# Two weight groups by turns: the first two column groups of the input projection advance together, a quarter of x at a time

## The chip, the core and the metric

One core of a Trainium2 chip runs the program. The metric is device microseconds of one execution, as the median of three runs, and less is better. TensorE (PE in the rows, PEld for its weight loads) does the matrix products, VectorE (DVE), ScalarE (ACT) and GpSimd (POOL) the elementwise work, and SyncE (SP) issues every load from memory.

## The reference, cut to what matters

The reference runs 256 tokens of 2048 features through two blocks of two layers each. Only the start of the first layer (`even_layer`) is touched here:

```
def even_layer(x, norm_g, w_in, ...):
    hn = rmsnorm(x, norm_g)               # x: 256 tokens x 2048 features
    proj = hn @ w_in                      # 2048 x 6144
    q, k, v, u, z_a, z_b = split(proj)    # 1024 columns each
    o_a = chunked_relpos_attention(q, k, v, rel_bias) * silu(z_a)
    y = gelu(s5_ssm(u, ...))              # state space model over u
    o_b = y * sigmoid(y @ w_glu + b_glu) * silu(z_b)
    return x + concat([o_a, o_b]) @ w_out
```

`rmsnorm` multiplies by the gain and divides by the root of the mean square over all 2048 features. The division is one factor for each token, so the kernel applies it to the finished product, not to x.

## The kernel before

**Jobs.** Every matrix product is cut into column groups of 512, and a group into jobs. A job holds two blocks of 128 rows of the weight for 512 columns: 0.5 MB, a tile `raw` of 128x1024 floats. `run` (line 267) goes through the list of jobs in order. A job's weight is loaded by SP, split by ACT into a high part (`hi`, line 214) and by DVE into the rest (`lo`, line 165), and multiplied by PE at line 420. PE does three products for each 128x128 block: x high times weight high, x low times weight high, x high times weight low, so 24 matmuls a job. Job i uses the tiles hi*i* and lo*i*. There are five `raw` buffers and four of `hi` and `lo`. The splits of a job stand up to two jobs ahead of its matmuls in the program (`ahead`, line 313).

**x.** x comes in four quarters of 512 features, and a group of the first layer goes through them in order, two jobs for each. When a job that needs a new quarter is prepared, ACT and DVE split that quarter too (`Act.split`, line 36: four pieces each, ACT `s<-s,e1g` at line 214 and DVE `s<-s,e1g,s` at line 176). Its hook `Norm.add` (line 444) then has ACT square the quarter and POOL add the square to the sum of squares (POOL `s<-s,s` 128x1024 at line 165).

**The norm.** After the fourth quarter the generator `norm_gen` takes over: two additions on DVE fold the sum, PE multiplies it by a matrix of ones (`b<-s,ones`, line 219), DVE forms the mean (`rsv`, line 172), ACT takes the logarithm and the exponential (`rst`, `rsy`, with a table load before each), and three more DVE instructions give the factor of each token, `rsy`.

**Accumulators.** A group's result gathers in one of two PSUM buffers (`ps_main`, bufs=2, names `mm...`). When the last job of a group is done, its `post` function is put on a list and called in `bg_step`; it empties the accumulator on DVE (`s<-mm,rsy`, line 165) and gives `'wait'` back as long as `norm_ok` isn't set. `run` forces background steps before a job while more than one `post` is outstanding. A third group reuses the first one's accumulator.

**Order.** All engines execute their instructions in the order in which the program lists them. Into the stream of jobs `bg_step` mixes background generators: the norm, the preparation of the S5 model (`s5pre`: small instructions of 128x32 on DVE, then additions and products of 128x512), the S5 blocks and the attention. Which instruction they add where follows from estimated costs, not from the chip. The first groups are u0, u1 (the S5 input), q0, k0, v0 and so on; u0 and u1 are also spread over partitions by eight small DMAs each (`stack`, line 726). The first loads are issued by the list `K.first`, where `None` stands for one `raw` and `load(i)` for quarter i of x.

Of the kernel before, what the change touches and what calls it, by code (L numbers as in the profile page):

```python
# [26 lines left out]
class Act:  # L27
    """256 columns of tokens for `n` blocks of 128 features, as two float32r parts."""
# [42 lines left out]
class Kern:  # L71
# [124 lines left out]
    def smax(self, out, a, b, acc):  # L196
        """out = -(a + b); acc = its least, the negative of the greatest of a + b"""
        self._ew('D', self._n(out))
        self.nc.vector.tensor_tensor_reduce(out=out, in0=a, in1=b, op0=OP.add, op1=OP.min,  # L199
                                            scale=-1.0, scalar=3.0e38, accum_out=acc)  # L200
# [26 lines left out]
    def lane(self, gens, width=1, prio=0, name=""):  # L227
        """a queue of (condition, generator maker), `width` of them at a time"""
        L = dict(q=list(gens), live=[], width=width, prio=prio, name=name)
        self.lanes.append(L)  # L230
        self.lanes.sort(key=lambda l: l['prio'])
        return L

    def bg_step(self, force=False):
# [9 lines left out]
        for L in list(self.lanes):  # L244
            while len(L['live']) < L['width'] and L['q'] and L['q'][0][0]():
                L['live'].append(L['q'].pop(0)[1]())
            for g in list(L['live']):
                if not force and max(self.busy.values()) > self.clock + self.SLACK and L['prio'] > 0:
                    return moved
                # not before what it waits for on another engine is done  # L250
# [16 lines left out]
    def run(self):  # L267
# [45 lines left out]
        def ahead(i):  # L313
            """the splits of the jobs after job i, as far as LOOK goes"""
# [12 lines left out]
        for i, j in enumerate(jobs):  # L327
            ahead(i)
            # a raw tile is free again once all of it is read
# [23 lines left out]
        n = 0  # L353
# [5 lines left out]
    def group(self, name, src, acts, orient, post, units, ready=None, bg=False):  # L359
        """one group of 512 columns: `units` is the list of (DRAM AP, kt count)"""  # L360
# [66 lines left out]
def kmap(acts):  # L427
    """k-tile index -> (Act, block in it)"""
    out = []
    for a in acts:  # L430
        out += [(a, i) for i in range(a.n)]
    return out


class Norm:
    """1 / sqrt(mean of squares + eps) for each token, the same on all partitions"""
# [7 lines left out]
    def add(self, src, cols=None):  # L444
        """src: a slot with four blocks of features"""
# [15 lines left out]
    def mean(self, out, extra=None):  # L461
        """generator: out = mean of squares (+ eps), then 1/sqrt"""
# [25 lines left out]
def rsqrt(K, y, v, t):  # L488
    """y = 1 / sqrt(v): a first value by exp(-ln(v) / 2), then a step of Newton"""
# [11 lines left out]
def together(*gens):  # L501
    """the operations of several chains by turns"""
# [9 lines left out]
def steps(n, gen):  # L512
    """n operations at a time"""
# [34 lines left out]
def sincos_ops(K, s, c, x, a, b, d):  # L548
    """sin and cos of x; a, b, d: scratch"""
# [31 lines left out]
    # n mod 4 in -2..2, then a turn by n quarters  # L581
# [10 lines left out]
    K.tt('D', z, z, n, OP.mult)                      # sine of the turn  # L592
    yield
    K.ts('D', r, r, -1.0, 1.0, OP.mult, OP.add)      # cosine of the turn
# [15 lines left out]
def evac_scaled(K, ps, rs, out=None):  # L610
    """a feature-major group times a row of tokens' factors"""
# [13 lines left out]
def evac_silu(K, ps, rs_half, done):  # L625
    """x times sigmoid(x): with h = x / 2 it is (tanh(h) + 1) h"""
# [12 lines left out]
def token_scales(K, rs, out):  # L639
    """generator: factors by token on partitions"""  # L640
# [8 lines left out]
def soft_rows(K, p, nm, sm, cols):  # L649
    """p holds -(s); exp(s - max) with its sums. cols: [(first, end)]"""  # L650
# [4 lines left out]
class E1:  # L655
    """relative-position attention in chunks beside an S5 state space model"""

    def __init__(self, K, D, x_src, out_norm):
# [12 lines left out]
        K.first += [None, lambda: load(0), None, lambda: load(1), None, None, lambda: load(2), lambda: load(3)]  # L671
# [26 lines left out]
    def build(self):  # L698
# [8 lines left out]
        def post_u(i):  # L707
            def f(ps):
                if not self.norm_ok or K.slots.free < 3:
                    return 'wait'  # L710
                # even tokens before odd ones
# [5 lines left out]
                def stack():  # L717
                    """both tokens of a pair on the partitions, for two tiles of states at a time"""
# [66 lines left out]
        def load_bias(hg):  # L785
            def gen():
                [s] = yield from K.gslots(1)
                K.nc.sync.dma_start(s, D['e1_bias'][hg])
                # keys of the chunk after the query's own are out of reach
# [138 lines left out]
        # the first half of y before the second  # L928
# [6 lines left out]
    def s5(self):  # L935
# [30 lines left out]
        def powers():  # L966
            """cosine and sine of 2, 4, .. 128 angles"""
# [9 lines left out]
        def coefs():  # L977
            """A, and the factor of B: (A - 1) / lambda"""
# [20 lines left out]
        def pre():  # L999
# [9 lines left out]
            def times(out, v, re, im, tm):  # L1009
                """a complex number for each state times its coefficients"""  # L1010
# [16 lines left out]
            # cosines and sines of 0, 2, .. 30 times each state's angle  # L1027
# [20 lines left out]
            # y takes the real part: the imaginary parts of C with their sign turned  # L1048
# [7 lines left out]
        def fill(e, pad, src, b):  # L1056
            """block b's coefficients, zero outside of each state's own channels"""
# [11 lines left out]
        def block(b):  # L1069
            def gen():  # L1070
# [7 lines left out]
                # the projections in, the channels of each tile's pairs of tokens on their own rows  # L1078
# [4 lines left out]
                # cosines and sines of 0, 2, .. 254 times each state's angle  # L1083
# [21 lines left out]
                # two tokens a step  # L1105
# [42 lines left out]
                # the even tokens' own inputs: C B  # L1148
# [28 lines left out]
                # gelu by tanh, twice its value  # L1177
# [22 lines left out]
        def yz(i):  # L1200
            def gen():
                # y times silu(z), a quarter of (2 y) (2 silu): y_t is 2 y; sigmoid's half is still to come
# [13 lines left out]
class Layer:  # L1216
    """what the layers share: the norm at their start and the sum with the residual at their end"""
# [15 lines left out]
    def begin(self):  # L1233
        """called when the projection out of the layer before starts"""
# [24 lines left out]
    def take(self, g, ps, xr):  # L1259
        """four blocks of the sum: the residual, and this layer's input"""  # L1260
# [13 lines left out]
def out_proj(K, D, wname, n, acts, xr, nxt, tag):  # L1274
    """xr: list of the residual's slots (filled by the time of use)"""
# [12 lines left out]
def attend(K, S_mm, bias, pv, out, left, done, heads=2):  # L1288
    """generator: two heads at a time, queries on partitions. S_mm(bank, e) emits the scores of head e
    (queries 0..127 with keys 0..127 in columns 0..127, queries 128..255 in columns 128..383)"""  # L1290
# [39 lines left out]
def log1p_ops(K, out, z, s, w, d):  # L1330
    """log(1 + z) for z in 0..1, by the series of atanh(z / (2 + z))"""
# [19 lines left out]
class O1(Layer):  # L1351
# [3 lines left out]
    def build(self):  # L1355
# [11 lines left out]
        # forget gates: 16 columns  # L1367
# [4 lines left out]
        def f_mm(raw, _):  # L1372
# [3 lines left out]
            # four blocks of rows at a time, on a quarter of the columns each  # L1376
# [4 lines left out]
        def f_post():  # L1381
# [6 lines left out]
            def gen():  # L1388
# [8 lines left out]
                K.stt(m, x, -1.0, x, OP.mult, OP.min)            # -|x|  # L1397
# [40 lines left out]
        # the first group before the gates, that the norm has its time  # L1438
# [69 lines left out]
class E2(Layer):  # L1508
    """HGRN2 beside sparse attention (whose blocks and window hold all of the tokens at this length)"""
# [20 lines left out]
    def norm_gen(self):  # L1530
        """the first block's last norm and this layer's, in one factor for each token"""
# [13 lines left out]
    def build(self):  # L1545
# [45 lines left out]
        def hgrn(i):  # L1591
            def gen():
# [6 lines left out]
                # pairs of tokens: (2i, 2i), (2i+1, 2i) and (2i+1, 2i+1) in one product  # L1599
# [112 lines left out]
    def nsa(self, g):  # L1712
# [54 lines left out]
        # the gates: 48 columns  # L1767
# [8 lines left out]
        def g_mm(raw, k0):  # L1776
# [4 lines left out]
            # two blocks of rows at a time, on half of the columns each  # L1781
# [8 lines left out]
        def g_post():  # L1790
# [6 lines left out]
            def gen():  # L1797
# [3 lines left out]
                # both halves' sum, tokens on the partitions  # L1801
# [9 lines left out]
                # no block is complete before token 31  # L1811
# [12 lines left out]
        # compressed keys and values: an MLP over blocks of 32 tokens  # L1824
        def c_mm(n, j, x):
            def f(raw, _):
# [6 lines left out]
                # even steps on the first half of the columns, odd ones on the second  # L1833
# [50 lines left out]
        # two steps after each group from the third on  # L1884
# [29 lines left out]
        def first_rows():  # L1914
            # the first 128 tokens' values, and the compressed ones, as two float32r parts
# [15 lines left out]
        def head(i, e):  # L1931
# [3 lines left out]
            def gen():  # L1935
# [19 lines left out]
                # the columns that no key has  # L1955
# [74 lines left out]
class O2(Layer):  # L2030
    """a short convolution and a gated linear recurrence"""
# [4 lines left out]
    def build(self):  # L2036
# [6 lines left out]
        # columns: four taps, their sum's bias, the gates' biases, lambda  # L2043
# [5 lines left out]
        def pre():  # L2049
# [3 lines left out]
            K.stt(v[0], lam, -1.0, lam, OP.mult, OP.min)                      # -|lambda|  # L2053
# [352 lines left out]
```

## Time and profile before

| what | value |
|---|---|
| median of 3 runs | 2395.09 us (2394.77 to 2395.71) |
| span of the profiled execution | 2394.8 us |
| PE busy | 2336.9 us, 98% of the span |
| DVE busy | 1585.9 us, 66% |
| ACT busy | 1152.5 us, 48% |
| POOL busy | 386.8 us, 16% |
| chain that ended last | PE 84%, DVE 8%, POOL 2%, issue 2%, ACT 2%, DMA 1% |

PE is busy nearly all of the time, and 84% of the chain that ended last is PE's. A shorter run can come only from the idle time of PE (58 us in all, span less busy time) or from its clock. The profiled execution's span is 0.3 us under the median; no other time is given for that execution. Matmuls overlap, so PE's pace is read from the distance between starts, not from the duration of one matmul.

### The profile page before, as it was taken

How to read it: one execution, taken by the hardware profiler on the slowest of the kernel's cores; microseconds unless marked ns; L12 is line 12 of the kernel's file. 1: busy time of each engine (PE TensorE's matmuls, PEld its weight loads, DVE VectorE, ACT ScalarE, POOL GpSimd, SP SyncE). 2: the span in 40 equal slices, each digit the busy share in tenths (PEclk: the TensorE clock that was granted, in tenths of full speed). 3: DMA queues.
4: the chain of work that ended last, by engine and by line, in shares of the span. 5: the costliest groups of instructions: out<-in, count | busy, mean ns of one | idle time of the engine just before them, and what ended most of it. 6: DMA issues, size and time to landing. Idle time of an engine off the chain costs nothing.

```text
span 2394.8 us, 47663 instructions
## 1 busy us (share of the span) xinstructions
PE 2336.9 (98%) x19906; PEld 2253.3 (94%) x19906; DVE 1585.9 (66%) x2409; ACT 1152.5 (48%) x1662; POOL 386.8 (16%) x320
## 2 busy tenths in 40 slices
PE   7999999999999999999999999999999999999997
PEld 7989998999999999989999999899999999999997
DVE  7978878675554545676758574566667446777764
ACT  5354454444444344543445443455555434666643
POOL 1111211010000000123324253101110000111210
PEclk9999999999999999999999999999999999999999
DMA  6544454555545555554544454554444555555453
GB/s 225 191 152 149 142 177 153 175 186 164 193 160 175 174 170 185 169 177 156 170 160 159 162 165 159 192 178 142 142 142 143 195 183 180 165 175 168 161 196 111
DMA packets 116167, 402.23 MB, mean 168 GB/s; under 512 B 14832, under 2 KB 17776, under 8 KB 115952
## 3 DMA queue, kind: packets, MB, share of 16 engines
q1 hardware_dynamic: 115952, 399.19, 50.7%
q8 instruction: 156, 2.56, 0.4%
q14 instruction: 59, 0.48, 0.1%
HBM read 396.00 MB, written 2.10 MB: 166 GB/s over the span
## 4 chain that ended last, share of the span: by engine, by line
PE 84%; DVE 8%; POOL 2%; issue 2%; ACT 2%; DMA 1%; DVEq 0%; SPq 0%; ACTq 0%; POOLq 0%
PE mm L420 75%; PE b L219 6%; DVE lo L165 3%; DVE s L165 2%; POOL s L165 2%; DVE s L194 1%; DVE s L176 1%; PE b L224 1%; PE b L420 1%; ACT s L214 1%; ACT hi L214 1%; DMA raw<-in_e_in 1%; PE b L1836 0%; DVE s L170 0%; DMA s<-in_e_bias 0%
## 5 line engine op out<-in xcount | busy, mean ns | idle before, releaser
L420 PE MATMUL mm<-s,hi 128*128 128x256 f32 x9984 | 1830.5, 285 | 10.4 <-ACT s L214 7.6
L420 PEld LDWEIGHTS mm<-s,hi 128*128 128x128 f32 x9984 | 1563.9, 193 | 18.3 <-ACT s L214 8.0
L420 PE MATMUL mm<-s,lo 128*128 128x256 f32 x4992 | 1418.6, 284 | 24.5 <-DVE lo L165 24.4
L165 DVE TENSOR_TENSOR lo<-raw,hi 128x1024 fp32r<-128x1024 f32 x730 | 934.0, 1294 | 622.2 <-ACT hi L214 620.4
L214 ACT ACTIVATE hi<-raw 128x1024 fp32r<-128x1024 f32 x730 | 756.9, 1054 | 646.1 <-PE mm L420 557.5
L420 PEld LDWEIGHTS mm<-s,lo 128*128 128x128 f32 x4992 | 960.8, 192 | 28.9 <-DVE lo L165 28.8
L165 POOL TENSOR_TENSOR s<-s,s 128x512 f32<-128x512 f32 (+1 forms) x128 | 273.9, 2154 | 1411.4 <-ACT s L214 586.9
L214 ACT ACTIVATE s<-s 128x1024 f32<-128x1024 f32 (+6 forms) x188 | 132.9, 713 | 263.3 <-DVE s L165 137.2
L420 PE MATMUL mm<-hi,s 128*128 128x512 f32 x768 | 244.6, 394 | 0.0
L219 PE MATMUL b<-s,s 128*32 128x32 f32 (+8 forms) x3008 | 175.0, 244 | 4.8 <-POOL s L186 2.1
L420 PEld LDWEIGHTS mm<-hi,s 128*128 128x128 f32 x768 | 145.0, 189 | 30.8 <-ACT s L214 0.3
L219 PEld LDWEIGHTS b<-s,s 128*32 128x32 f32 (+2 forms) x2976 | 148.3, 135 | 23.4 <-POOL s L186 2.5
L420 PE MATMUL mm<-lo,s 128*128 128x512 f32 x384 | 150.5, 392 | 1.6 <-DVE lo L165 1.6
L214 ACT ACTIVATE s<-b 128x384 f32<-128x384 f32 (+6 forms) x135 | 57.2, 462 | 134.9 <-PE b L219 92.7
L165 DVE TENSOR_TENSOR s<-s,s 128x512 f32<-128x512 f32 (+8 forms) x134 | 85.8, 666 | 45.7 <-ACT s L214 44.5
L420 PEld LDWEIGHTS mm<-lo,s 128*128 128x128 f32 x384 | 72.6, 189 | 16.7 <-DVE lo L165 2.4
L176 DVE SCALAR_TENSOR_TENSOR s<-s,s 128x1024 f32<-128x1024 f32 (+3 forms) x76 | 82.6, 1089 | 3.1 <-ACT s L214 2.2
L214 ACT ACT_TABLE_LOAD x44 | 56.5, 1283 | 16.1 <-DVE s L176 14.7
L204 DVE COPY_PREDICATED s<-hmask,b 32x64 f32<-32x64 int32 (+1 forms) x144 | 36.0, 250 | 30.4 <-PE b L219 26.6
L214 ACT ACTIVATE s<-s,nsam 128x15 f32<-128x15 f32 (+2 forms) x96 | 37.6, 394 | 36.0 <-DVE nsam L199 36.0
L170 POOL TENSOR_SCALAR s<-alibi 128x256 f32<-128x256 f32 x16 | 17.8, 1111 | 212.3 <-PE b L219 174.1
L186 POOL MEMSET s<- 128x512 f32 (+7 forms) x65 | 25.8, 410 | 123.3 <-DMA s<-in_e_bias 59.1
(148 smaller groups left out, 966.6 us busy)
## 6 DMA issues: line engine op xcount, KB each, us to landing
raw<-in_e_in SPq DMA_DIRECT2D x336, 512.0 KB, 4.1
raw<-in_o_in SPq DMA_DIRECT2D x208, 512.0 KB, 4.0
raw<-in_e_out SPq DMA_DIRECT2D x80, 512.0 KB, 4.2
raw<-in_o_out SPq DMA_DIRECT2D x72, 512.0 KB, 4.4
raw<-in_e_outa SPq DMA_DIRECT2D x16, 512.0 KB, 3.6
raw<-in_o_rg SPq DMA_DIRECT2D x10, 512.0 KB, 3.7
raw<-in_e_glu SPq DMA_DIRECT2D x8, 512.0 KB, 3.8
raw<-in_e_cmp SPq DMA_DIRECT2D x8, 512.0 KB, 5.1
```

The lines of the kernel that those rows point to most:

```text
L165: self._eng(e).tensor_tensor(out, a, b, op=op)
L170: self._eng(e).tensor_scalar(out, a, s1, None, op0=op0)
L176: self.nc.vector.scalar_tensor_tensor(out, a, s, b, op0=op0, op1=op1)
L186: self._eng(e).memset(out, v)
L194: self.nc.vector.tensor_tensor_scan(out, d0, d1, init, op0=OP.mult, op1=OP.add)
L204: self.nc.vector.copy_predicated(out, mask, a)
L214: self.nc.scalar.activation(out, a, func, scale=scale, **kw)
L219: self.nc.tensor.matmul(out, l, r, start=start, stop=stop, skip_group_check=True, **kw)
L224: self.nc.tensor.transpose(out, a, self.ident[:p, :p])
L420: self.nc.tensor.matmul(out, l, r, start=start, stop=stop, skip_group_check=True)
```

## The change

The list of jobs of the first two groups is rearranged, and the list of first loads with it. Comments and docstrings that went away are left out of this diff.

```
-        K.first += [None, lambda: load(0), None, lambda: load(1), None, None, lambda: load(2), lambda: load(3)]
+        K.first += [None, lambda: load(0), None, None, None, lambda: load(1), None, lambda: load(2), lambda: load(3)]
...
         for g, (n, i, o) in enumerate(order):
             K.group(f"e1.{n}{i}", None, acts, o, posts[n](i), units('e1_in', g))
 
+        n = 4 // K.JK
+        j = K.jobs[:8 * n]
+        K.jobs[:8 * n] = [j[g * 4 * n + u * n + i] for u in range(4) for g in range(2) for i in range(n)]
```

JK is 2, so n is 2. Before, jobs 0 to 7 are u0 on the four quarters of x and jobs 8 to 15 are u1. Now jobs 0 and 1 are u0 on the first quarter, 2 and 3 u1 on the first quarter, 4 and 5 u0 on the second, and so on to jobs 14 and 15, u1 on the fourth. Both accumulators are open from job 2 on. The second, third and fourth quarter of x are needed at jobs 4, 8 and 12 instead of 2, 4 and 6. u0 is complete after job 13 instead of job 7; u1 after job 15 in both. Job 16, the first of q0, takes over u0's accumulator in both.

On PE, around the matrix of ones (`b`) and the first matmul of job 16 (`mm53`, in u0's accumulator). Before, where `mm45` is u1:

```order
L420 MATMUL mm45_508<-s32_148,lo8_425 128x256
L219 MATMUL b46_533<-s34_158,ones_79 128x256
L420 MATMUL mm45_508<-s32_148,hi9_464 128x256
...
L420 MATMUL mm45_508<-s42_347,lo15_720 128x256
L420 MATMUL mm53_833<-s32_148,hi16_761 128x256
```

Now, where `mm39` is u1:

```order
L420 MATMUL mm39_262<-s43_586,lo14_675 128x256
L219 MATMUL b49_769<-s34_158,ones_79 128x256
L420 MATMUL mm39_262<-s43_586,hi15_709 128x256
...
L420 MATMUL mm39_262<-s43_586,lo15_710 128x256
L420 MATMUL mm53_852<-s32_148,hi16_739 128x256
```

The ones stood seven jobs ahead of job 16 and now stand one job ahead of it.

On DVE, from the mean to the emptying of u0's accumulator. Before (`mm38` is u0):

```order
L165 TENSOR_TENSOR lo11_544<-raw11_360,hi11_543 128x1024
L172 TENSOR_SCALAR rsv5_86<-b46_533 128x256
L165 TENSOR_TENSOR rst6_87<-rsv5_86,rsy7_88 128x256
L176 SCALAR_TENSOR_TENSOR rst6_87<-rst6_87,rsy7_88 128x256
L176 SCALAR_TENSOR_TENSOR rsy7_88<-rst6_87,rsy7_88 128x256
...
L165 TENSOR_TENSOR lo13_630<-raw13_428,hi13_629 128x1024
L165 TENSOR_TENSOR s47_659<-mm38_187,rsy7_88 128x4x128x2
```

Now (`mm35` is u0, `mm39` u1; `s46` to `s50` belong to S5):

```order
L165 TENSOR_TENSOR lo17_775<-raw17_599,hi17_774 128x1024
L172 TENSOR_SCALAR rsv5_86<-b49_769 128x256
...
L176 SCALAR_TENSOR_TENSOR rsy7_88<-rst6_87,rsy7_88 128x256
L165 TENSOR_TENSOR s47_669<-s46_668,s11_98 128x512
L165 TENSOR_TENSOR s48_670<-s46_668,s11_98 128x512
L165 TENSOR_TENSOR s47_669<-s47_669,s48_670 128x512
L165 TENSOR_TENSOR lo18_814<-raw18_637,hi18_813 128x1024
...
L165 TENSOR_TENSOR s48_670<-s50_821,s5pw13_100 128x32 x2
...
L165 TENSOR_TENSOR s50_821<-s50_821,s48_670 128x32x4 x2
L165 TENSOR_TENSOR s51_842<-mm35_174,rsy7_88 128x4x128x2
L165 TENSOR_TENSOR s52_844<-mm39_262,rsy7_88 128x4x128x2
```

The mean now stands behind lo17 instead of lo11, and the forced background steps put 18 S5 products and additions of 128x32 to 128x128 between the token factors and the emptying of u0, where before there were two scalings by a half, one `lo` and some small S5 instructions. From the 2939th PE instruction on (job 108) the order of the two kernels is the same.

## Rows read from the trace of the kernel before

**Rows 1.** Waits of PE, 0 to 60 us: total, times, longest.

```profile
PE mm L420 <- DVE lo L165: 4.1, 2, 2.6
```

**Rows 2.** PE's timeline: start and duration in us, in brackets idle time before.

```profile
19.39 0.40 PE L420 MATMUL mm<-s,hi 128*128 128x256 f32 x2
21.25 0.39 PE L420 MATMUL mm<-s,lo 128*128 128x256 f32 x1 [1.46 <-DVE lo L165]
...
24.93 0.39 PE L420 MATMUL mm<-s,hi 128*128 128x256 f32 x1 [0.66 <-DVE s L176]
...
30.82 0.58 PE L420 MATMUL mm<-s,lo 128*128 128x256 f32 x1 [2.64 <-DVE lo L165]
...
43.69 0.60 PE L219 MATMUL b<-s,ones 128*128 128x256 f32 x2
...
64.49 0.40 PE L420 MATMUL mm<-s,hi 128*128 128x256 f32 x2
...
75.41 0.39 PE L420 MATMUL mm<-s,lo 128*128 128x256 f32 x1 [1.83 <-DVE lo L165]
```

**Rows 3.** Two stretches; the figure behind POOL's count (0.52) is the granted clock.

```profile
31.20:34.40 3.20, 3.20 (x17) 3.20 (x17) 3.20 (x11) 0.00 (x0) 0.00 (x0) 0.52 0.77 192
137.00:140.20 3.20, 3.20 (x9) 2.50 (x8) 3.20 (x4) 2.01 (x5) 0.00 (x0) 0.52 0.29 60
```

**Rows 4.** DVE's timeline, 14 to 35 us.

```profile
14.97 1.67 DVE L176 SCALAR_TENSOR_TENSOR s<-s,e1g,s 128x256 fp32r<-128x256 f32 x4
16.55 2.63 DVE L172 TENSOR_SCALAR s<-s 128x32 f32<-128x32 f32 x2
...
22.25 3.82 DVE L176 SCALAR_TENSOR_TENSOR s<-s,e1g,s 128x256 fp32r<-128x256 f32 x4
25.98 3.41 DVE L176 SCALAR_TENSOR_TENSOR s<-s 128x32 f32<-128x32 f32 x6
...
31.78 1.22 DVE L165 TENSOR_TENSOR lo<-raw,hi 128x1024 fp32r<-128x1024 f32 x1
32.92 1.67 DVE L176 SCALAR_TENSOR_TENSOR s<-s,e1g,s 128x256 fp32r<-128x256 f32 x4
34.50 0.28 DVE L176 SCALAR_TENSOR_TENSOR s<-s 128x32 f32<-128x32 f32 x2
```

**Rows 5.** POOL's timeline: the first two of three additions of squares.

```profile
16.42 2.50 POOL L165 TENSOR_TENSOR s<-s,s 128x1024 f32<-128x1024 f32 x1 [13.79 <-ACT s L214]
22.07 2.52 POOL L165 TENSOR_TENSOR s<-s,s 128x1024 f32<-128x1024 f32 x1 [3.15 <-ACT s L214]
```

**Rows 6.** Timeline of DVE and ACT: the norm and the emptying of u0.

```profile
45.52 0.42 DVE L172 TENSOR_SCALAR rsv<-b 128x256 f32<-128x256 f32 x1
47.70 0.42 ACT L214 ACTIVATE rsy<-rst 128x256 f32<-128x256 f32 x1
49.41 0.41 DVE L165 TENSOR_TENSOR s5pw<-s5pw,s 128x32 f32<-128x32 f32 x2
54.24 2.03 DVE L165 TENSOR_TENSOR s<-mm,rsy 128x1024 f32<-128x1024 f32 x1
```

**Rows 7.** DVE's timeline: three S5 instructions; 18 small ones' start; what follows them.

```profile
61.10 2.01 DVE L165 TENSOR_TENSOR s<-s,s 128x512 f32<-128x512 f32 x3
...
76.50 0.71 DVE L165 TENSOR_TENSOR s<-s,s5pw 128x32 f32<-128x32 f32 x4
...
80.15 2.35 DVE L165 TENSOR_TENSOR lo<-raw,hi 128x1024 fp32r<-128x1024 f32 x2
```

**Rows 8.** SP's timeline: the eight DMAs that spread u0.

```profile
58.68 6.64 SPq L726 DMA_DIRECT2D s<-s  x8
```

**Rows 9.** Waits of PE, 136 to 400 us.

```profile
PE mm L420 <- DVE lo L165: 3.2, 3, 1.4
PE b L224 <- POOL s L182: 2.2, 1, 2.2
PE b L219 <- POOL s L186: 2.1, 1, 2.1
```

## Prediction

> **What bounds the kernel now.** I read the page first: PE is busy for 98% of the span, so only its idle time and its clock can give or cost something. Then I read PE's waits in the first 60 us [rows 1], and PE's timeline to see where they lie [rows 2]. After the first load PE stops three times in the first group, u0: 1.46, 0.66 and 2.64 us, 4.76 together. Each ends when DVE delivers a `lo` or a piece of x. After the longest of them PE's clock is granted at 0.52 in the mean of a stretch of 3.2 us, the level of 1.2 GHz, and PE gets 17 matmuls through it [rows 3]. At its usual pace it would be 26: from the ones at 43.69 to job 16 at 64.49 lie 171 PE instructions, 0.122 us each [rows 2], which makes 2.9 us a job. The stretch lasts 3.4 us by the distance of the starts, so it costs about 1.5 us.
>
> Next I read DVE around these waits [rows 4] with POOL beside it [rows 5]. Two instructions of 128x32 take 2.63 us, where a stretch without POOL gives 0.13 each: 11.0 us from 34.50 [rows 4] to 45.52 [rows 6] hold five `lo` of 1.14 (31.78 to 32.92), two foldings of the sum of about 1.1 together (an estimate, from a third of the triple of [rows 7] and half of that) and 32 small ones. Four pieces of x take 3.82 instead of 1.67, six small ones 3.41 instead of 0.8. Each of the three begins just after POOL began to add squares, 2.50 us [rows 5]; the third addition is of the same kind. So each addition cost DVE 2.2 to 2.6 us, 7.1 us together, and this is a good part of why `lo` came late.
>
> **The change, part by part.** No instruction's work goes or comes: 16 jobs, 16 loads, three additions, one norm remain. Three things move.
>
> (a) The quarters of x are needed at jobs 4, 8 and 12 instead of 2, 4 and 6. DVE then has four jobs (11.6 us of PE) for one quarter: four `lo` at 1.14 (4.6), four pieces 1.6 (32.92 to 34.50), some 30 small ones (4) and one blocked addition of at most 2.5 make 12.7 at the worst against 11.6, which the splits that stand two jobs ahead cover for three quarters; before it was the same less two `lo` and half of the small ones, 8.4 against 5.8. The three waits in u0 go, and the half-clock stretch with them. Job 3 starts at 19.39 [rows 2] as before, jobs 3 to 15 and the ones take 13 x 2.9 + 0.25 = 37.9, and PE would reach job 16 at 57.3, 7.2 earlier than its 64.49. The first loads only follow the new need: raw 2 and 3 ahead of the second quarter. Bounds: nothing to 7.2 us; but it is a gain only if job 16 can start then.
>
> (b) Job 16 can't. It writes into u0's accumulator, which DVE must empty first, with factors that come out of the norm, and the norm needs the last quarter of x. Before, u0 was emptied from 54.24 to 56.27 [rows 6], 8.2 us ahead of job 16. Now the chain is this. The ones stand behind job 14 on PE, at 57.3 - 2.9 - 0.25 = 54.1, with 0.6 of duration 54.7. DVE, in order, reaches the mean after 14 `lo` (lo4 to lo17, 16.0), three quarters of x (4.7), 81 small ones (10.5), three triples of 128x512 (5.8, [rows 7] less the overlap) and the two foldings (1.1): 38.1 us. lo4 can start at 16.5 to 17.9: lo2 is done at 14.97 [rows 4], then 14 small ones and lo3 take 2.9, less up to 1.4 because 0.5 MB of x no longer lie ahead of the weight (an estimate from the stretch's load rate; I take 16.5). That gives 54.6 for the mean without any blocking. With it, 0 to 7.1 more; the additions again meet pieces of x and small ones on DVE, but not at the same points, so I take two thirds, 4.9. The mean starts at 59.5, and what PE does before it, waits included, sets nothing any more.
>
> From the mean to the next free slot of DVE it was 3.9 us (45.52 to 49.41, with ACT's logarithm, table load and exponential in it [rows 6]): 63.4. Then, as the program lists them, one triple 1.95, lo18 1.14, two scalings of 128x256 (0.42 at most each, I take 0.6 together), the 18 S5 instructions 3.65 (76.50 to 80.15, [rows 7]) and the emptying itself 2.03 [rows 6]: 72.8. PE stands still from about 57.3 to 72.8, and job 16 starts 8.3 later than before. Queued behind job 16's first matmul are only PE's own jobs 16 and on; ACT's hi20 and on wait for PE in turn, so nothing else gets ahead.
>
> After this stop PE restarts at the lower clock. Before, 2.64 us of idle brought one half-clock stretch, 1.5 us. Nothing before, away from the start, shows a stop of 15 us. Bounds 0 and 3 (two such stretches); I take 1.5, by the nearest row.
>
> The Trainium skill, "SBUF — State Buffer", section "Who interferes with whom", says that a DVE instruction with two SBUF inputs contends with a GpSimd instruction that reads SBUF, and the one that issues second waits it out in full. The rows above agree, with 2.2 to 2.6 us for an addition of 2.5. By that rule all three additions of the new order block in full, 7.4 us in place of my 4.9, and the sum would be 2.5 us larger.
>
> (c) The 16 small DMAs for u0 and u1 are issued together now. Before, SP was tied up for 6.64 us by the first eight [rows 8], the next weight came late, and PE waited 1.83 us at 75.41 [rows 2]. Now eight jobs' weights are issued ahead of them in SP's order, through job 23; both sets end 13.3 us after u0's emptying, at about 86, and job 24 starts not before 72.8 + 8 x 2.9 = 96. This wait goes with its restart: -1.9. If a load then takes over 10 us, it stays.
>
> Sum: +8.3 + 1.5 - 1.9 = +7.9 us on the span of 2394.8: 2402.7, and with the 0.3 by which the median is above the span, 2403.0. The part after 96 us I leave as it is: the S5 blocks move by some jobs against the weights up to job 108, but the waits there hang on the same chains of DVE and POOL.
>
> **Rivals.** A, DVE isn't blocked: the additions fall beside instructions that don't mind. The mean is then at the ones, 54.7, all else 4.8 earlier: +3.1, 2398.2. For it: the new order spaces the additions 11.6 us apart. Against it: in [rows 4] three of three blocked.
>
> B, the other side: S5's new place clears the later waits. From 136 to 400 us PE waits 7.5 us for S5's operands and late `lo` [rows 9], and one such stop is followed by 0.52 of the clock [rows 3]; three groups of them would make 4.5. S5's blocks stand earlier against the weights now, by up to some 140 matmuls in the PE order. Were all of these waits to go, 7.9 - 12.0 = -4.1: 2391.0, not slower. It decides from about 8 us on. Against it: between the first S5 transposes and the first S5 output lie twelve jobs and ten `lo` in both orders, so I see no more room there than before.
>
> C, job 16 doesn't wait, since a free accumulator is found. Then -7.2 - 1.9 = -9.1: 2386.0. Against it: two buffers, both open from job 2 on.
>
> D, S5's new place makes a further group of waits like that at 136 us, 2.1 and 1.5: +11.5, 2406.6. Nothing speaks for or against it.
>
> **How the numbers follow.** This kernel's measurement can tell 0.2%, 4.8 us, from no change. The forecast with its own range (blocking 3 to 7.1, clock 0 to 3: 2399.6 to 2406.7) has 0.52, D 0.08, A 0.17, B 0.19 and C 0.04. Slower by over 0.2% are most of the forecast and D: 0.58. Within are A, two thirds of B and the low end of the forecast: 0.32. Faster are C and the part of B that comes with A: 0.10. The range runs from 2393.5, which takes in A and half of B, to 2408.0, which takes in D with some blocking more.
>
> **What would show it.** Right: no PE wait over 0.7 us between 19 and 54 us and no half-clock stretch there; then one wait of 12 to 17 us on DVE's emptying (`s<-mm,rsy`) right behind the second group, half clock after it, no wait of 1.8 us for job 19, and `rsv` on DVE starting 4 to 6 us after the ones. Wrong: `rsv` within 1 us of the ones (A), PE without a long wait before q0 (C), or the waits of 136 to 400 us gone (B). The forecast as a whole is wrong if job 16 starts before 66 us.

## The result, and the profile after

| | kernel before | changed kernel |
|---|---|---|
| median | 2394.93 us (2390.95 to 2395.71, 4 runs) | 2419.21 us (2418.12 to 2420.26, 4 runs) |
| span of the profiled execution | 2394.8 us | 2417.0 us |
| PE busy | 2336.9 us | 2339.1 us |
| idle time of PE (span less busy) | 57.9 us | 77.9 us |

The changed kernel is slower: ratio 1.0101, 95% interval 1.0087 to 1.0116, or 24.3 us. The forecast of slower was right. 2403.0 was not, and the range, up to 2408, does not hold the time. Of the 22.2 us between the two spans 20.0 are idle time of PE, and 2.2 are more busy time for the same 19906 matmuls.

**The start.** PE's waits in the changed kernel, 0 to 60 us: total, times, longest.

```profile
PE mm L420 <- DVE lo L165: 2.3, 4, 0.7
PE mm L420 <- DVE s L176: 0.6, 2, 0.4
```

The three waits of [rows 1, 2] are gone; what is left are six short ones. Now the timeline of the changed kernel from the ones to job 16, PE first, then DVE (start and duration in us, in brackets idle time before).

```profile
55.99 0.60 PE L219 MATMUL b<-s,ones 128*128 128x256 f32 x2
60.01 0.28 PE L420 MATMUL mm<-s,lo 128*128 128x256 f32 x1
74.62 0.77 PE L420 MATMUL mm<-s,hi 128*128 128x256 f32 x2 [14.33 <-DVE s L165]
...
61.46 0.42 DVE L172 TENSOR_SCALAR rsv<-b 128x256 f32<-128x256 f32 x1
68.91 0.71 DVE L165 TENSOR_TENSOR s<-s,s5pw 128x32 f32<-128x32 f32 x4
72.55 3.76 DVE L165 TENSOR_TENSOR s<-mm,rsy 128x1024 f32<-128x1024 f32 x2
```

The mean (`rsv`) starts 5.5 us after the ones, the 18 small S5 instructions stand ahead of the emptying, and job 16 starts at 74.62 instead of 64.49 [rows 2], 10.1 us later. The clock in four stretches of the changed kernel (busy time and count of PE, PEld, DVE, ACT and POOL, then the granted clock, DMA share and GB/s):

```profile
31.20:34.40 3.20, 3.03 (x25) 2.83 (x25) 3.13 (x9) 1.06 (x1) 0.00 (x0) 1.00 0.30 87
74.60:79.60 5.00, 4.98 (x24) 5.00 (x25) 4.76 (x8) 0.00 (x0) 0.00 (x0) 0.51 0.32 79
206.60:212.30 5.70, 5.01 (x21) 4.72 (x22) 5.49 (x7) 3.02 (x4) 2.65 (x2) 0.50 0.41 132
316.70:321.80 5.10, 5.10 (x22) 4.92 (x23) 3.57 (x10) 3.42 (x10) 0.00 (x0) 0.50 0.31 106
```

The half-clock stretch at 31 us [rows 3] is gone. In its place PE is granted 0.51, the 1.2 GHz level, after the long wait, and two more such stretches lie at 207 and 317 us.

**After 96 us.** In the two traces the last of PE's matmuls that differs is the 3396th, in job 108, at 406 us of the kernel before. PE's waits in the changed kernel, 136 to 400 us, the window of [rows 9].

```profile
PE b L219 <- DVE e1m L199: 6.6, 2, 5.4
PE b L219 <- issue: 5.2, 2, 3.9
PE mm L420 <- DVE lo L165: 2.4, 3, 1.2
PE mm L420 <- ACT hi L214: 1.2, 2, 0.6
PE b L219 <- POOL s L165: 0.9, 1, 0.9
```

They add up to 16.3 us. In the kernel before all waits of this window are 8.4 us, of which [rows 9] shows the three largest, 7.5. And they are other waits: the two rows for POOL there are gone, and the two at the top here are new. "issue" means that the profile gives no releaser for PE. The timeline of the engines around the first of them, 206 us, shows one:

```profile
197.89 0.42 SPq L792 DMA_DIRECT2D s<-in_e_bias  x1
203.00 1.02 POOL L186 MEMSET s<- 64x256 f32 x3 [4.36 <-DMA s<-in_e_bias]
203.79 1.90 ACT L214 ACTIVATE s<-s 64x128 f32<-64x128 f32 x6 [10.28 <-POOL s L186]
205.72 3.90 ACT L214 ACTIVATE hi<-raw 128x1024 fp32r<-128x1024 f32 x4
205.79 0.44 PE L219 MATMUL b<-s,s 128*32 128x32 f32 x16 [3.90 <-issue]
206.83 0.80 PE L420 MATMUL mm<-s,hi 128*128 128x256 f32 x2 [0.59 <-ACT hi L214]
208.09 0.58 PE L420 MATMUL mm<-s,lo 128*128 128x256 f32 x1 [0.46 <-DVE lo L165]
```

POOL's row holds three memsets. The first masks the attention bias and must wait until that bias has come by DMA, at 203 us. The other two clear the tiles of an S5 block and do not need the bias; they only stand behind it on POOL. ACT's six copies fill these tiles, ACT's `hi` stands behind the copies, and PE's 16 matmuls of 128x32 read them: 3.9, 0.6 and 0.5 us of waiting, and half clock after it. Around 317 us:

```profile
310.69 2.34 POOL L165 TENSOR_TENSOR s<-s,s 128x1024 f32<-128x1024 f32 x1 [5.24 <-DVE s L176]
310.84 2.47 DVE L165 TENSOR_TENSOR s<-s 128x256 f32<-128x256 f32 x1
313.34 0.42 ACT L214 ACTIVATE s<-s 128x256 f32<-128x256 f32 x1 [5.13 <-DVE s L165]
314.74 1.32 DVE L165 TENSOR_TENSOR lo<-raw,hi 128x1024 fp32r<-128x1024 f32 x1 [1.43 <-ACT hi L214]
316.67 1.65 PE L219 MATMUL b<-s,s 128*128 128x128 f32 x4 [5.39 <-DVE e1m L199]
```

POOL multiplies the attention output by its gate. The DVE instruction that began 0.15 us later, a step of an S5 block's gelu, takes 2.47 us; ACT's tanh, ACT's `hi`, DVE's `lo`, the row maxima of the attention and PE follow in a chain.

### The profile page after: what moved, and what is told of

It reads as the page before. It is cut to its first block, busy times and chain, and to the rows that moved or that the text cites. A ratio compares the mean times of both kernels' runs of the same rounds, so it can differ in the third digit from the quotient of the medians.

```text
span 2417.0 us, 47650 instructions
## 1 busy us (share of the span) xinstructions
PE 2339.1 (97%) x19906; PEld 2253.2 (93%) x19906; DVE 1586.4 (66%) x2409; ACT 1152.7 (48%) x1662; POOL 384.1 (16%) x320
## 4 chain that ended last, share of the span: by engine, by line
PE 81%; DVE 4%; POOL 2%; issue 1%; ACT 1%; DMA 0%; DVEq 0%; ACTq 0%; SPq 0%; POOLq 0%
PE mm L420 73%; PE b L219 6%; POOL s L165 2%; DVE lo L165 2%; PE b L420 1%; DVE s L165 1%; PE b L224 1%; ACT s L214 1%; DVE s L194 1%; ACT hi L214 1%; DVE s L176 1%; PE b L1840 0%; PE mm L219 0%; DMA s<-in_e_bias 0%; DVE s L199 0%
## 5 line engine op out<-in xcount | busy, mean ns | idle before, releaser
L219 PE MATMUL b<-s,s 128*32 128x32 f32 (+9 forms) x3008 | 177.3, 245 | 16.2 <-issue 6.7
L186 POOL MEMSET s<- 128x512 f32 (+8 forms) x65 | 25.5, 406 | 146.2 <-DMA s<-in_e_bias 74.9
```

What stands on the lines that cost most here:

```text
L186: self._eng(e).memset(out, v)
L219: self.nc.tensor.matmul(out, l, r, start=start, stop=stop, skip_group_check=True, **kw)
```

## The experiments

The ratios are to the kernel before, run on the same chip beside each kernel (its medians there: 2394.6 to 2396.2 us). Experiments 1 to 4 share a chip, 5 to 8 a second and 9 to 11 a third; 12 has a fourth, and the changed kernel of the result was timed apart from them. A difference of two experiments of different sets is therefore given against the kernel before as well, and 2 to 3 us can lie within the intervals. All experiments but the fourth need the S5 and attention steps at chosen jobs. For that the class `Kern` is replaced by one that takes these steps from a list. Filled with a kernel's own places it gives that kernel's own order on every engine.

```
-    K = Kern(tc, ctx, slots=SLOTS)
+    K = Pinned(tc, ctx, slots=SLOTS)
...
+PINNED = [
+    (45,0,0), (45,0,1), (51,0,0), (51,0,1), (53,0,0), (53,0,1), (55,0,0), (57,0,0), (57,0,1), (59,0,0), (59,0,1),
...
+        while self.pin and abs(self.pin[0][0]) <= self.pos:
+            p, name, k = self.pin[0]
```

An entry is twice the job's number plus one, the lane (0 is S5, 1 attention) and which of its blocks. By the traces, experiments 5, 6 and 12 then differ from the changed kernel only in the instructions that were moved, and 9 and 10 likewise from the kernel before.

| kernel | median us | ratio, 95% interval |
|---|---|---|
| 1 changed, S5 steps of before | 2405.97 | 1.0040 (1.0027 to 1.0053) |
| 2 before, S5 steps of changed | 2416.85 | 1.0087 (1.0074 to 1.0101) |
| 3 as 1, prompt emptying | 2399.38 | 1.0014 (1.0005 to 1.0023) |
| 4 changed, old order of loads | 2420.98 | 1.0104 (1.0088 to 1.0119) |
| 5 changed, bias mask later | 2409.01 | 1.0052 (1.0039 to 1.0064) |
| 6 changed, gate on DVE | 2417.31 (1 run) | |
| 7 as 3, two quarters by turns | 2396.00 | 0.9999 (0.9990 to 1.0008) |
| 8 as 1, squares on DVE | 2401.93 | 1.0021 (1.0013 to 1.0030) |
| 9 before, squares on DVE | 2391.44 | 0.9985 (0.9977 to 0.9994) |
| 10 as 9, bias mask later | 2389.77 | 0.9976 (0.9967 to 0.9985) |
| 11 as 7, both edits of 10 | 2390.86 | 0.9978 (0.9969 to 0.9987) |
| 12 changed, 5 and 6 together | 2406.05 | 1.0044 (1.0031 to 1.0058) |

**1. The changed start with the S5 steps where they were.** Expected:

> The changed kernel, with every step of the S5 and attention generators put at the job and in the order that it has in the kernel before (from job 22 on the engines then run the same order of instructions as before). Theory T (the loss has two parts: about 11 us at the start, from the wait for u0's accumulator, and about 12 us after 96 us, from the new place of the S5 steps): the start is as in the changed kernel, with one wait of about 14 us near 60 us, the waits of 3.9 us at 206 and 5.4 us at 317 are gone, and the time is 2406 (2403 to 2409). Rival R (the later loss comes from the late start itself, whatever the order of the steps): the time stays at 2417 to 2420.

Measured 2405.97, as theory T has it. The long wait is there (14.34 us, job 16 at 74.02), and from 136 to 400 us this kernel's PE waits are those of [rows 9] again, 8.3 us in all:

```profile
PE mm L420 <- DVE lo L165: 2.1, 3, 1.0
PE b L219 <- POOL s L186: 2.1, 1, 2.1
PE b L224 <- POOL s L182: 1.8, 1, 1.8
PE b L219 <- ACT s L214: 1.4, 1, 1.4
```

So the start costs 10.7 us (2405.97 less 2395.31), and the other 13 to 14 us (24.3 less 10.7; 13.2 by 2419.21 less 2405.97) come from where the S5 and attention steps stand, not from being late.

**2. The start of before with the S5 steps of the changed kernel.** Expected:

> The kernel before, with its jobs and loads, and with the S5 and attention steps at the jobs that they have in the changed kernel (those of jobs 18 to 35 drawn together into 22 to 35, since the S5 coefficients aren't there earlier). Theory T: the start is as before, new waits as in the changed kernel come near 195 and 305 us, and the time is 2407 (2404 to 2411). Rival R: 2395 (2393 to 2397).

Measured 2416.85, 10 us over T's value. The new waits are at their places: 3.45, 0.59 and 0.46 us at 202 us and 2.66 and 4.03 us near 303 and 313. But PE waits 6.14 us for the first S5 outputs at 126 us, where the kernel before waits 2.08 and the changed kernel 1.52. That it comes from the steps drawn together is likely and not shown. The run speaks against R and measures nothing.

**3. u0 emptied at once.** The token factors no longer give way to other generators before the emptying:

```
-            yield from self.norm.mean((r['v'], r['t'], r['y']))
+            yield from self.norm.mean((r['v'], r['t'], r['y']), last=True)
...
             self.norm_ok = True
+            d, K.delayed = K.delayed, []
+            K.delayed = [f for f in d if f() == 'wait'] + K.delayed
```

Not shown: with `last`, `mean` leaves out the `yield` behind the factors.

> The first of these kernels, and in it u0's accumulator is emptied right behind the token factors, ahead of the S5 additions, lo18 and the 18 small S5 instructions that stood between them (about 7 us of DVE). Theory T (job 16 waits for nothing but this emptying): job 16 starts at about 68 instead of 74.6 us, PE's wait falls from 14.3 to 7.5 to 8 us, and the time is 6 to 7 us under the first kernel's, about 2399.5. Rival: lo18 or the S5 steps, now later, hold PE up right after, and at most 2 us are won (2404 or more).

Measured 2399.38, 6.6 us under experiment 1. DVE and PE in this kernel:

```profile
66.64 1.92 DVE L165 TENSOR_TENSOR s<-mm,rsy 128x1024 f32<-128x1024 f32 x1
68.71 0.77 PE L420 MATMUL mm<-s,hi 128*128 128x256 f32 x2 [7.66 <-DVE s L165]
```

Job 16 starts 0.15 us after the emptying ends. Of the long wait, half (14.34 less 7.66) was DVE work that could have come later.

**4. The order of the loads undone.**

```
-        K.first += [None, lambda: load(0), None, None, None, lambda: load(1), None, lambda: load(2), lambda: load(3)]
+        K.first += [None, lambda: load(0), None, lambda: load(1), None, None, lambda: load(2), lambda: load(3)]
```

> The changed kernel with the first loads in the order of before (the second quarter of x ahead of the third and fourth weight); the order of the jobs stays changed. Theory T (the order of the jobs does all of it): 2419 (2417 to 2421), the same start of the long wait within 1 us. Rival (the order of the loads has a share): over 2 us away from 2419, with PE's waits for weights before 20 us, since two weights come one transfer later.

Measured 2420.98, with a wait of the same length, 14.35 us up to 76.43 us. ACT at the weight of job 4:

```profile
17.77 1.06 ACT L214 ACTIVATE hi<-raw 128x1024 fp32r<-128x1024 f32 x1 [3.24 <-DMA raw<-in_e_in]
```

The order of the jobs does it. But the wait begins and ends 1.8 us later than in the changed kernel, where T had its start within 1 us: ACT waits 3.24 us for this weight, and lo4 starts at 18.86 us, where it starts at 17.18 in the changed kernel. So the new order of the loads saves some 1.7 us at the start; in the time (2420.98 against 2419.21) that is less than these intervals can tell.

**5. POOL does not stand at the bias.**

```
-                K.ms('G', s.rearrange("p (h k) -> p h k", h=4)[0:64, :, 192:256], -1e30)
...
+                if 2 * hg + j // 2 not in masked:
+                    masked.add(2 * hg + j // 2)
+                    K.ms('G', bias[0:64, :, 192:256], -1e30)
                 S = yield from K.gbanks(2)
```

> The changed kernel with all S5 and attention steps where it has them, but POOL's memset of the attention bias, which waits for the DMA of that bias, is issued in the first attention step that uses the bias instead of right behind the load. Theory T (at 206 us PE waits because POOL stands at this memset, and behind it in POOL's order the memset of an S5 block, ACT's copies into it and ACT's hi wait in turn): the waits of 3.9, 0.6 and 0.5 us at 206 to 209 us and the half-clock stretch behind them go, 5 + 3.4 us, and most of the 1.3 us at 307 us, where POOL stands at the next bias; the time is 2410 (2408 to 2413). Rival (POOL's or ACT's own work on the S5 block is what is late): the wait at 206 us keeps 3 us or more, and the time stays at 2416 to 2420.

Measured 2409.01, 10.2 us under the changed kernel; against the kernel before on each chip, 24.3 us fall to 12.8. The timeline of this kernel at the place of the wait at 206 us:

```profile
198.31 0.53 POOL L186 MEMSET s<- 128x512 f32 x1
199.58 0.32 POOL L186 MEMSET s<- 128x256 f32 x1 [0.74 <-DVE s L165]
198.88 1.91 ACT L214 ACTIVATE s<-s 64x128 f32<-64x128 f32 x6 [5.35 <-POOL s L186]
203.18 0.39 PE L420 MATMUL mm<-s,lo 128*128 128x256 f32 x1 [0.58 <-DVE lo L165]
206.56 0.77 POOL L186 MEMSET s<- 64x256 f32 x2
```

The S5 memsets come at 198.3 instead of after 203, ACT's copies with them, and the mask at 206.6 waits for nothing and is waited for by nobody. One `lo` wait of 0.58 is left of 5.0 us, and the clock from 203 to 209 us is 1.00.

**6. The gate on DVE.**

```
-                K.tt('G', self.oa_t[hg], self.oa_t[hg], st['za'][hg], OP.mult)
+                K.tt('D', self.oa_t[hg], self.oa_t[hg], st['za'][hg], OP.mult)
```

> The changed kernel with the product of the attention output and its gate on DVE instead of POOL (two instructions of 128x1024). Theory T (in the stop at 317 us, POOL's product of 2.34 us blocks a DVE instruction of the S5 block, which takes 2.47 us where it takes 0.28 elsewhere, and ACT's tanh, hi, DVE's lo and the row maxima follow in a chain): the DVE instruction takes 0.3 us, the product 1.2 us on DVE, and PE's wait falls from 5.4 to about 4.3 us. Rival (the chain is held by something else, POOL's copies behind the product): the wait stays over 5 us.

The DVE instruction takes 0.42 us (as this shape does elsewhere in the changed kernel too; 0.28 is what a TENSOR_SCALAR of 128x256 takes), the product 1.22, and PE's wait falls to 1.74, further than expected; the wait of 1.33 us at 307 us, nine us earlier, grows to 2.05. The two waits trade: experiment 4, with the changed kernel's order on every engine, has 2.35 and 3.91 us there. Together they are 6.7 us in the changed kernel, 6.3 in experiment 4 and 3.8 here. One run of 2417.31 tells no difference in time from 2419.21.

**12. Both edits in the changed kernel.**

> The changed kernel with all S5 and attention steps where it has them, the memset of the attention bias in the first step that uses it, and the gate's product on DVE. Theory T (what the later part cost is these two places: POOL standing at the bias, and POOL's product that blocks DVE; with the steps where the kernel before has them it was 2406.0): the wait of 3.2 us at 305 us falls to 1.5 or less, the half-clock part behind it shrinks, and the time comes to within 2 us of that, 2406.5 (2405 to 2408.5). Rival (there is a third cause in the new place of the S5 steps): 2409 or more.

Measured 2406.05, within 0.1 us of experiment 1; against the kernel before on each chip it is 11.4 us and 10.7. Two rows of this kernel:

```profile
299.60 0.42 DVE L165 TENSOR_TENSOR s<-s 128x256 f32<-128x256 f32 x1
303.29 0.92 PE L219 MATMUL b<-s,s 128*128 128x128 f32 x4 [0.95 <-DVE e1m L199]
```

PE's wait of 3.16 us in experiment 5 is 0.95 here, and the clock behind it is 1.00 from 303.3 to 306.8 us, where experiment 5 has 0.57 from 305.1 to 308.6. So, as far as these intervals tell, the two places hold all that the new position of the S5 steps cost. How much the second place costs in time is not told apart from noise: 12.8 us over the kernel before in experiment 5, 11.4 in 12.

**7. Two quarters by turns.**

```
-        K.jobs[:8 * n] = [j[g * 4 * n + u * n + i] for u in range(4) for g in range(2) for i in range(n)]
+        K.jobs[:8 * n] = [j[g * 4 * n + u * n + i] for u in range(2) for g in range(2) for i in range(n)] + j[2 * n:4 * n] + j[(4 + 2) * n:]
```

> The third kernel (u0 emptied promptly, S5 and attention steps where the kernel before has them), with only the first two quarters of x by turns, and then u0 and u1 each with its last two quarters: x is needed at jobs 4, 8 and 10, and u0 ends with job 11. Theory T (job 16 waits for the chain from the last quarter through the norm to the emptying of u0): the mean on DVE comes 4 to 6 us earlier than the 61.5 of the changed kernel, PE's wait at job 16 falls from 7.7 to 1 to 3 us, and the time to 2393.5 (2391 to 2396), which is under the kernel before. Rival (two quarters in a row block DVE again as in the kernel before): waits on lo or on pieces of x of 2 us or more between 30 and 45 us come back and the time is 2397 or more.

Measured 2396.00: no difference from the kernel before, so the forecast of faster failed. DVE and PE:

```profile
57.44 0.42 DVE L172 TENSOR_SCALAR rsv<-b 128x256 f32<-128x256 f32 x1
...
39.46 0.58 PE L420 MATMUL mm<-s,lo 128*128 128x256 f32 x1 [3.00 <-DVE lo L165]
63.97 0.47 PE L420 MATMUL mm<-s,hi 128*128 128x256 f32 x2 [2.54 <-ACT hi L214]
66.86 0.58 PE L420 MATMUL mm<-s,lo 128*128 128x256 f32 x1 [2.41 <-DVE lo L165]
```

The mean comes 4.0 us earlier, as expected. But the rival's wait of 3.0 us is back, and around the emptying the weights' `hi` and `lo` are late instead: DVE has the same work to do.

**8 and 9. The squares added on DVE**, in experiment 1 and in the kernel before:

```
-            K.tt('G', self.acc, self.acc, sq, OP.add)
+            if self.name == 'n1':
+                K._ew('G', K._n(sq))
+                K.nc.vector.tensor_tensor(self.acc, self.acc, sq, op=OP.add)
```

(The planner still books the addition on POOL, so that the order stays.)

> The first of these kernels (changed kernel, S5 steps where the kernel before has them), with the three additions of squares on DVE instead of POOL, all else in the same order. Theory T (each POOL addition of 2.5 us holds up one DVE instruction by 2.2 us, 6.6 us together, and DVE's lateness is what sets the mean): DVE loses 6.6 us of waiting and gains three additions of about 1.15, the mean comes at 58.2 instead of 61.5, PE's wait falls from 14.3 to about 11.5 us, the time from 2406 to 2403. Rival (the blocking isn't on the path to the mean): the mean comes later, by up to 3.5 us, and the time is 2406 to 2410.

Measured 2401.93, 4.0 us under experiment 1 (5.7 us over the kernel before on its chip, where experiment 1 has 10.7), although DVE has 3.4 us more work to do: three additions, each followed 1.13 us later by the next instruction. The mean comes at 58.40, where experiment 1 has 60.86:

```profile
58.40 0.42 DVE L172 TENSOR_SCALAR rsv<-b 128x256 f32<-128x256 f32 x1
71.56 0.77 PE L420 MATMUL mm<-s,hi 128*128 128x256 f32 x2 [14.33 <-DVE s L165]
```

The forecast of 11.5 us for the wait is wrong: it stays at 14.33, and PE comes to it 2.4 us earlier too. PE's arrival was set by DVE's `lo` as well, so the length of the wait says nothing of how late the emptying is; its end does. Counted from lo4 (17.30 us here, 16.66 in experiment 1) the mean comes 3.1 us sooner, about the 6.6 less 3.4 of theory T. Job 16 starts 2.5 us sooner (71.56 against 74.02); the rest of the 4.0 us the start does not show.

> The kernel before with its own order everywhere, and the three additions of squares on DVE instead of POOL. Theory T (each POOL addition held up DVE by 2.2 to 2.6 us, and this is what the three waits in u0 come from): DVE loses 7.1 us of waiting and gains 3 x 1.15; PE's waits of 1.5, 0.7 and 2.6 us in u0 fall to about 1.2 us together, and the half-clock stretch at 31 us goes (1.5): 2390 (2388 to 2392.5). Rival (the waits come from the pieces of x and lo that stand close together, not from POOL): the waits stay over 4 us together, 2394 to 2397.

Measured 2391.44, 4.0 us under the kernel before. The stretch that [rows 3] shows at 0.52:

```profile
31.00:34.00 3.00, 2.05 (x17) 1.85 (x16) 3.00 (x11) 1.06 (x1) 0.00 (x0) 1.00 0.86 324
```

PE's waits in u0 are 0.27, 0.45 and 0.95 us now, where [rows 2] has 4.76 together.

**10 and 11. Both edits, without and with turns.** The edits are those of 5 and 9.

> The kernel before with the squares added on DVE, and the memset of the attention bias moved into the first attention step that uses it. Theory T: as the kernel without the second edit, and in addition the wait of 2.2 us at 249 us, where POOL had stood at the bias until 245 us with the copies of an S5 block behind it, goes with the half-clock stretch behind it (1.7): 3 to 4 us under the kernel with the first edit alone, 2386.5 (2384 to 2389). Rival: another engine's work is late there by nearly as much, at most 1 us is won by the second edit.

Measured 2389.77: the fastest kernel here, under both kernels of this study. The wait of 2.2 us on POOL in [rows 9] is gone, but the second edit wins 1.7 us, less than these intervals can tell, and not 3 to 4: the profiled execution of experiment 9 had a wait of 1.85 us there, and no half clock behind it.

> The kernel with two quarters by turns, prompt emptying and the S5 steps of before, with both edits (squares on DVE, bias memset later). Theory T: the wait of 3.0 us at 40 us goes (two blocked instructions within six jobs), the mean comes about 3 us earlier, the waits of 5 us at 64 to 67 us fall to 2 to 5, the stop at 250 us goes with its clock: 2396 less 3.0, 1 and 3.9, 2388 (2385 to 2391); no faster than the kernel before with both edits, since that one has no wait at job 16. Rival (the turns are worth something once DVE isn't blocked): under 2385.

Measured 2390.86: the 3.0 us at 40 us are gone, 3.5 and 2.1 us remain, ending at 60.5 and 63.4 us. With DVE unblocked the turns are worth nothing that these runs can tell, either way (2389.77 without them).

## Why the prediction was wrong

- **(a) The three waits in u0 go:** right, with the half-clock stretch. PE reached job 16 at 60.3 and not 57.3, held up by DVE in several small waits, which cost nothing because the emptying ended later.
- **(b) Job 16 waits for u0's emptying:** right in mechanism and chain. The mean came 5.5 us after the ones in a forecast of 4 to 6, and from the mean to job 16 it was 13.2 us where I had 13.3 (59.5 to 72.8). The length of the wait, 14.33 us in 12 to 17, is partly luck: both of its ends came late. From lo4 to the mean DVE was busy for 43.73 of 44.28 us, so its own work sets the mean:

```profile
17.18:61.46 44.28, 40.55 (x324) 39.07 (x322) 43.73 (x120) 21.56 (x27) 8.58 (x6) 1.00 0.61 214
```

Mis-sized is POOL's blocking of DVE. I took 4.9 us, two thirds of 7.4; here are the three additions on POOL and the DVE instructions that overlap them in the changed kernel:

```profile
18.87 2.60 POOL L165 TENSOR_TENSOR s<-s,s 128x1024 f32<-128x1024 f32 x1 [16.21 <-ACT s L214]
27.76 2.92 POOL L165 TENSOR_TENSOR s<-s,s 128x1024 f32<-128x1024 f32 x1 [6.28 <-ACT s L214]
40.08 2.47 POOL L165 TENSOR_TENSOR s<-s,s 128x1024 f32<-128x1024 f32 x1 [9.40 <-ACT s L214]
...
18.33 3.83 DVE L176 SCALAR_TENSOR_TENSOR s<-s,e1g,s 128x256 fp32r<-128x256 f32 x4
28.34 2.39 DVE L176 SCALAR_TENSOR_TENSOR s5mag<-s5mag,s 128x32 f32<-128x32 f32 x1
40.20 3.43 DVE L165 TENSOR_TENSOR lo<-raw,hi 128x1024 fp32r<-128x1024 f32 x1
```

Against 1.67, 0.13 and 1.22 elsewhere that is 2.2 each, 6.6 together: the mean came 2.0 us after my 59.5, of which this is 1.7. Of the rest, lo4 came 0.7 us after my 16.5, and DVE's other work was 0.4 us less than my 38.1. Experiments 8 and 9 show that the blocking was on the path. Rival A is out. The rule that I weighed and did not take, the Trainium skill, "SBUF — State Buffer", section "Who interferes with whom" (the second of the two waits the first one out), put the mean at 62.0; the trace has 61.46 and agrees with it rather than with my two thirds. But the sentence that I drew on does not cover all of [rows 4]: taken singly, the first blocked instruction there reads one tensor only.

```profile
16.55 2.41 DVE L172 TENSOR_SCALAR s<-s 128x32 f32<-128x32 f32 x1
```

- **The clock after it:** 24 matmuls took 5.0 us where 24 at 0.122 take 2.9, so 2.1 us in place of 1.5, within its bounds of 0 to 3. (The 1.5 itself is a little high: 3.4 us less 17 matmuls at 0.122 is 1.3.)
- **(c) The wait of 1.83 us at 75 us goes:** right; from job 16 to 98 us PE does not wait once.
- The start then sums to 10.1 + 2.1 - 1.8 = 10.4, where experiment 1 measures 10.7 and I had 7.9. With this the time would have been 2405.5, inside the range.
- **"The part after 96 us I leave as it is":** this is the step that failed. I put nothing on it, and it held 13 to 14 of the 24 us. I argued that the S5 steps keep their chains. They do, but on POOL and DVE, which take their instructions in the listed order, they got other neighbours: an S5 block's memsets fell right behind a memset that waits for a DMA (10.2 us, experiment 5), and a gelu step fell beside POOL's gate product (5.39 us of waiting at 317 us; worth 1 to 3 us of time by experiments 5 and 12, within their intervals). Rival D was of this kind, but I priced it by one existing wait, 3.6 us, gave it 0.08 and wrote that nothing spoke for it. Something could have been looked up. On POOL, the order of the changed kernel shows the mask directly ahead of an S5 block's memset at three places, that of before at two, and the trace of before already has one such place, the POOL wait of 2.2 us in [rows 9]. Such a place need not cost anything: of the three in the changed kernel, at 165, 203 and 304 us, PE waits behind the last two (3.9 and 1.3 us). Rival B, that S5's new place would help, went the other way.

## What to carry to other kernels

When a planner mixes background work into a stream, a change at the start can move much of it: here all up to job 108. Compare the order of every engine to the end of the moved part, and look on each for an instruction that waits for a DMA with other work queued behind it: what it costs depends on its neighbours, here from nothing to 5 us of waiting. Two groups by turns need their last inputs and the factor for the emptying before the next group wants an accumulator; count the emptying engine's work back from there. Each addition that was given to GpSimd cost VectorE 2.2 us here, against 1.13 us for doing it itself.

## What the runs showed of the hardware that was not expected

The same stop of PE, 2.06 to 2.08 us ahead of the first S5 outputs, was followed by half clock in six profiled executions (the kernel before, and experiments 3, 7, 8, 10, 11: mean clock 0.55 to 0.63 over 3.5 us) and by full clock in two (experiments 1 and 9). The stretch behind it in experiment 9 and then in experiment 10, where PE had waited 2.07 and 2.06 us:

```profile
132.80:136.30 3.50, 3.50 (x16) 2.89 (x17) 2.90 (x4) 2.64 (x6) 0.00 (x0) 1.00 0.17 43
```

```profile
133.20:136.70 3.50, 3.50 (x9) 2.78 (x10) 2.92 (x4) 2.62 (x6) 0.00 (x0) 0.55 0.17 41
```

From these outputs to the beginning of PE's next stop it is 108.7 us in experiments 1 and 9 and 110.3 in the kernel before and experiments 3, 7 and 8, so the half clock cost 1.6 us where it came. It did not come each time, and what decides that these runs do not show: each is one execution of its kernel.
